# Head sums, low-rank products and a row broadcast as float32r passes of two parts, in a hybrid decoder trunk

## The chip, the cores and the metric

The kernel runs on one core of one Trainium2 chip. The metric is the device time of one execution in microseconds (us); the time before is a median over runs, and the profile is of one further execution.

## The reference

The program is a decoder trunk of two layers over 512 tokens of width 1024. Each layer is half a SwiGLU block, a mixer, and another half of a SwiGLU block; layer 0 mixes with differential attention and RWKV-7, layer 1 with sparse attention (NSA) and an mLSTM. Cut to what the change touches, in float32:

```python
# RWKV-7: 8 heads of 64; the low-rank terms, the normed key, the bonus and the norm of the output
w = -softplus(-(w0 + tanh(wl) @ w2)) - 0.5          # wl: (T, 64), w2: (64, 512)
a = sigmoid(a0 + al @ a2)                           # al: (T, 64), a2: (64, 512)
g = sigmoid(gl) @ g2                                # gl: (T, 128)
kk = kk * rsqrt(sum(kk * kk, over the head) + 1e-12)
S = S * w_t - (S kk) (kk a) + v k                   # state per head, step by step over T
y = (y - mean(y, over the head)) * rsqrt(var(y, over the head) + eps) * ln_w + ln_b
bonus = sum(r * k * r_k, over the head) * v
out = (y + bonus) * g

# mLSTM: 4 heads; each needs its running maximum m (one row of T numbers) on every partition
sqk = (q k) * exp(b_s - b_r + li_r - m_s)
```

## The kernel before

The kernel is written with a tile framework: the program issues instructions in an order of its own, a scheduler reorders them by priority and by modelled times, hands out buffers, and sets all waits. `tc.high_priority(n)` moves a block of instructions n places ahead. Activations lie with channels on the 128 partitions and the 512 tokens along the free axis, so a "512-column matmul" has all tokens as columns.

Nearly all of the work is weight products. `mm3` (L245 to L249) takes a float32 product apart: weights and activations are each split in a high part, rounded to float32r, and a low part, the rest; three float32r passes (high by high, high by low, low by high) are summed in PSUM. The split of weights is `split_weights` (ScalarE copy L275, VectorE subtraction L276). The small products of the mixers are matmuls on plain float32 operands.

Layer 0's mixer is `mix0` (from L685). It handles the eight RWKV heads as four pairs `hp` (two heads fill 128 partitions). `ORDER0` lists the steps: `in` (projections of r, k, v by `shifted`), `prep` (`rwkv_prep`), `inv` (`rwkv_inverse`, a triangular inverse by levels; the next pair's `prep` runs between its levels), `chain` (`rwkv_chain`), `din` and `attn` (differential attention), `out` (output projection). `AHEAD` moves `inv` 200 and `chain` 700 places ahead; the projections, the attention and `out` fill TensorE between their steps.

In `rwkv_prep` the two low-rank products of a pair (64 rows each: L764 on partitions 0 to 63, L768 on 64 to 127) read the tile `wag`, of two buffers, in which three DMAs put a pair's columns of w2, a2 and g2. A sum over a head is a matmul with the 0/1 matrix `blk` (128x128): L792 (squares of the key), L809 (bonus), and in the tail of `rwkv_chain` L963 (mean) and L967 (variance). L811 reads the product of L809 once the pair before has given up its `bonus`. `rwkv_chain` goes through eight chunks of 64 tokens: for each, two state products (L925), an addition (L927), two products (L931), two copies (L932, L933), two products (L937) and the new state (L945), which is kept in the tile `S` of seven buffers until the outputs (L956); `Sq` has the decayed old state (L944). Products take PSUM from the banks of a stream: `pi` (two banks) in `prep` and `inv`, `pc` (one) in `chain`, `mm` (two) in the projections.

`self.temp()` is a ring of three tiles of 128x512 for short-lived values: `shifted` uses one, `diff_in` one for each of q, k, v and one more while `rope` swaps rows by four DMAs (L631).

In layer 1, `mix1_gates` leaves the running maximum of the four mLSTM heads in `fm` (4 x 512), and `mlstm_head` copies a head's row to all 128 partitions by a product with a column of the identity (L1165, four rows).

## Time and profile before

| | us |
|---|---|
| median of 3 runs | 2134.4 |
| lowest and highest of them | 2131.72, 2139.27 |
| the profiled execution | 2132.14 |
| its span in the trace | 2130.3 |

TensorE is busy for 99% of the span, VectorE for 78%, ScalarE for 51%; the granted clock is 0.998 of full speed on average. A busy share counts time in which at least one instruction is under way. Matmuls are pipelined: one that takes 0.39 us can end 0.23 us after the one before it, so what an operation costs TensorE is read from the distance between the ends, not from its duration.

### The profile page before, as it was taken

How to read it: one execution, taken by the hardware profiler on the slowest of the kernel's cores; microseconds unless marked ns; L12 is line 12 of the kernel's file. 1: busy time of each engine (PE TensorE's matmuls, PEld its weight loads, DVE VectorE, ACT ScalarE, POOL GpSimd, SP SyncE). 2: the span in 40 equal slices, each digit the busy share in tenths (PEclk: the TensorE clock that was granted, in tenths of full speed). 3: DMA queues.
4: the chain of work that ended last, by engine and by line, in shares of the span. 5: the costliest groups of instructions: out<-in, count | busy, mean ns of one | idle time of the engine just before them, and what ended most of it. 6: DMA issues, size and time to landing. Idle time of an engine off the chain costs nothing.

```text
span 2130.3 us, 35226 instructions
## 1 busy us (share of the span) xinstructions
PE 2102.7 (99%) x14028; PEld 1787.9 (84%) x14028; DVE 1668.6 (78%) x2824; ACT 1086.3 (51%) x1917; POOL 68.4 (3%) x70
## 2 busy tenths in 40 slices
PE   9999999999999999999999999999999999999998
PEld 7999998776667679999989999997777768999997
DVE  7888886777778798878859787876687867888885
ACT  7544445534434465444446454453368846544444
POOL 1000002000000020000010000001000001000000
PEclk9999999999999999999999999999999999999999
DMA  5333334221121033333323333336421023333331
GB/s 145 106 105 106 103 100 125 69 59 46 43 58 34 31 99 98 116 94 102 107 90 99 106 102 108 95 97 165 120 59 36 25 62 88 97 115 96 102 107 70
DMA packets 306965, 190.94 MB, mean 90 GB/s; under 512 B 20054, under 2 KB 302448, under 8 KB 306800
## 3 DMA queue, kind: packets, MB, share of 16 engines
q1 hardware_dynamic: 305680, 187.59, 30.2%
q8 instruction: 110, 1.80, 0.4%
q0 software_dynamic: 1120, 1.11, 0.3%
q14 instruction: 55, 0.45, 0.1%
HBM read 181.32 MB, written 2.10 MB: 86 GB/s over the span
## 4 chain that ended last, share of the span: by engine, by line
PE 93%; DVE 3%; ACT 2%; DMA 1%; issue 1%; POOL 0%; SPq 0%; DVEq 0%; ACTq 0%; POOLq 0%
PE ps L518 33%; PE ps L247 15%; PE ps L248 15%; PE ps L249 15%; PE ps L849 2%; PE ps L1379 1%; PE ps L831 1%; PE ps L1376 1%; PE ps L1229 1%; DVE wlo L276 1%; PE ps L1182 1%; PE ps L1360 1%; PE ps L1035 1%; PE ps L952 0%; PE ps L1361 0%
## 5 line engine op out<-in xcount | busy, mean ns | idle before, releaser
L275 ACT ACTIVATE whi<-wraw 128x1024 fp32r<-128x1024 f32 (+2 forms) x367 | 320.5, 876 | 307.9 <-PE ps L248 197.3
L276 DVE TENSOR_TENSOR wlo<-wraw,whi 128x1024 fp32r<-128x1024 f32 (+2 forms) x367 | 368.6, 1006 | 75.7 <-ACT whi L275 72.2
L518 PE MATMUL ps<-xi,shi 128*128 128x256 f32 x1800 | 330.6, 283 | 1.4 <-ACT g L529 1.4
L518 PEld LDWEIGHTS ps<-xi,shi 128*128 128x128 f32 x1800 | 280.6, 192 | 1.8 <-ACT g L529 1.8
L248 PE MATMUL ps<-hlo,whi 128*128 128x512 f32 (+1 forms) x716 | 276.9, 387 | 0.0
L247 PE MATMUL ps<-hhi,whi 128*128 128x512 f32 (+1 forms) x716 | 276.8, 387 | 0.0
L249 PE MATMUL ps<-hhi,wlo 128*128 128x512 f32 (+1 forms) x716 | 276.2, 386 | 0.0
L518 PE MATMUL ps<-xi,slo 128*128 128x256 f32 x900 | 254.4, 283 | 0.0
L247 PE MATMUL ps<-xhi,whi 128*128 128x512 f32 x600 | 245.7, 411 | 0.3
L248 PE MATMUL ps<-xlo,whi 128*128 128x512 f32 x600 | 243.4, 406 | 0.4 <-DVE xlo L294 0.4
L249 PE MATMUL ps<-xhi,wlo 128*128 128x512 f32 x600 | 243.0, 405 | 0.0
L501 ACT ACTIVATE shi<-sum 128x1024 fp32r<-128x1024 f32 x150 | 158.5, 1059 | 136.0 <-DVE sum L496 89.1
L502 DVE TENSOR_TENSOR slo<-sum,shi 128x1024 fp32r<-128x1024 f32 x150 | 183.2, 1222 | 29.0 <-ACT shi L501 28.2
L518 PEld LDWEIGHTS ps<-xi,slo 128*128 128x128 f32 x900 | 172.6, 192 | 0.0
L518 PE MATMUL ps<-xlo,whi 128*128 128x256 f32 x600 | 169.6, 283 | 0.0
L518 PE MATMUL ps<-xhi,whi 128*128 128x256 f32 x600 | 169.4, 283 | 0.0
L518 PE MATMUL ps<-xhi,wlo 128*128 128x256 f32 x600 | 169.3, 283 | 0.0
L495 DVE TENSOR_TENSOR sum<-wraw 128x512 f32<-128x512 f32 x150 | 99.1, 689 | 88.1 <-DMA wraw<-in_ffa_up_dram 45.6
L249 PEld LDWEIGHTS ps<-hhi,wlo 128*128 128x128 f32 x716 | 134.5, 188 | 27.3
L247 PEld LDWEIGHTS ps<-hhi,whi 128*128 128x128 f32 x716 | 134.7, 188 | 25.7
L248 PEld LDWEIGHTS ps<-hlo,whi 128*128 128x128 f32 x716 | 134.7, 188 | 24.9
L247 PEld LDWEIGHTS ps<-xhi,whi 128*128 128x128 f32 x600 | 113.6, 190 | 28.3 <-issue 3.8
(422 smaller groups left out, 4198.0 us busy)
## 6 DMA issues: line engine op xcount, KB each, us to landing
wraw<-in_ffb_gate_dram SPq DMA_DIRECT2D x44, 512.0 KB, 3.8
wraw<-in_ffb_up_dram SPq DMA_DIRECT2D x44, 512.0 KB, 3.9
wraw<-in_ffa_gate_dram SPq DMA_DIRECT2D x43, 512.0 KB, 3.8
wraw<-in_ffa_up_dram SPq DMA_DIRECT2D x43, 512.0 KB, 3.9
wraw<-in_ffa_down_dram SPq DMA_DIRECT2D x48, 384.0 KB, 3.1
wraw<-in_ffb_down_dram SPq DMA_DIRECT2D x48, 384.0 KB, 3.1
wraw<-in_ab_w_in_dram SPq DMA_DIRECT2D x26, 512.0 KB, 3.9
wraw<-in_cd_w_in_dram SPq DMA_DIRECT2D x18, 512.0 KB, 3.8
```

Source lines behind the costliest of these rows:

```text
L247: mm(out, w[0], x[0], start=start, stop=False)
L248: mm(out, w[0], x[1], start=False, stop=False)
L249: mm(out, w[1], x[0], start=False, stop=stop)
L275: nc.scalar.activation(h, raw, AF.Copy)
L276: nc.vector.tensor_sub(l, raw, h.bitcast(F32))
L495: nc.vector.tensor_add(t[:, 0], *first)
L501: nc.scalar.activation(hi, t, AF.Copy)
L502: nc.vector.tensor_sub(lo, t, hi.bitcast(F32))
L518: nc.tensor.matmul(out, a[:, j], b, start=first and i + j == 0, stop=i + j == 5, skip_group_check=True)
L831: mm(p[:, c * P:(c + 1) * P], BK[h, 4 * q + c, :], AR[h, 4 * q + c, :], start=True, stop=True)
L849: mm(p[h, c * LC:(c + 1) * LC], lhs[h, c, :], rhs[h, c, :], start=True, stop=True)
L1035: mm(po[:, :P], et[:, j, :], v[:, j, :], start=j == 0, stop=j == i)
```

## The change

`head_sums` replaces the float32 matmuls with `blk` (L792, L809 and, for pairs 0 to 2, L963 and L967): the operand is split in two float32r parts in two tiles of `temp()`, and two float32r passes with a float32r `blk` add up in PSUM. `blk` holds zeros and ones, which a float32r operand holds exactly, so it has one part. Pair 3 keeps the float32 matmuls in its chain. The low-rank products are three float32r passes for each half, of `wr` (w2 and a2 of the pair) split in `w2hi`, `w2lo` and of the activations, split once. g2 goes to a tile of its own. The RWKV states go into columns of `BT` that are done with, and `S`, `Sq`, `wag` and `wa` are dropped. For the mLSTM the four rows of m are split in float32r, high parts on rows 0 to 3 and low parts on rows 32 to 35 of a 64-row tile of zeros, and one float32r pass with a two-ones column `sel` gives the broadcast.

```diff
+    def head_sums(self, p, t):
+        nc = self.nc
+        hi, lo = [self.temp().bitcast(FR) for _ in range(2)]
+        nc.scalar.activation(hi, t, AF.Copy)
+        nc.vector.tensor_sub(lo, t, hi.bitcast(F32))
+        for part in (hi, lo):
+            nc.tensor.matmul(p, self.blk, part, start=part is hi, stop=part is lo)
...
# mix0: blk is loaded apart from the other constants, and rounded
+            blk = self.temp()[:, :P]
+            self.nc.sync.dma_start(blk, a["c_blk"])
+            self.blk = self.tile("blk", (P, P), FR)
+            self.nc.scalar.activation(self.blk, blk, AF.Copy)
...
# rwkv_low
-        wa = self.shifted(6 * T, 12, "wa")
+        wa = self.shifted(6 * T, 12, "rkv")
...
+        hi, lo = [self.tile(n, dt=FR) for n in ("wahi", "walo")]
+        nc.scalar.activation(hi, wa, AF.Copy)
+        nc.vector.tensor_sub(lo, wa, hi.bitcast(F32))
+        return (hi, lo), gl
...
# rwkv_prep
-        wag = R["wag"] = self.tile("wag", (P, 2, P))
-        nc.sync.dma_start(wag[:64, 0, :], self.a["rwkv_w2"][0, :, cs])
-        nc.sync.dma_start(wag[64:, 0, :], self.a["rwkv_a2"][0, :, cs])
-        nc.sync.dma_start(wag[:, 1, :], self.a["rwkv_g2"][0, :, cs])
-        p = self.psum("pi")
-        mm(p, wag[:64, 0, :], wa[:64, :], start=True, stop=True)
-        sig = self.tile("tr")
-        self.act(sig, p, AF.Sigmoid, bias=self.vec("w0", hp))
-        p = self.psum("pi")
-        mm(p, wag[64:, 0, :], wa[64:, :], start=True, stop=True)
-        av = self.tile("tr")
-        self.act(av, p, AF.Sigmoid, bias=self.vec("a0", hp))
+        g2 = R["g2"] = self.tile("g2", (P, P))
+        wr, whi, wlo = self.tile("wr", (P, P)), self.tile("w2hi", (P, P), FR), self.tile("w2lo", (P, P), FR)
+        nc.sync.dma_start(wr[:64], self.a["rwkv_w2"][0, :, cs])
+        nc.sync.dma_start(wr[64:], self.a["rwkv_a2"][0, :, cs])
+        nc.sync.dma_start(g2, self.a["rwkv_g2"][0, :, cs])
+        nc.scalar.activation(whi, wr, AF.Copy)
+        nc.vector.tensor_sub(wlo, wr, whi.bitcast(F32))
+        ps = [self.psum("pi") for _ in HALF]
+        for i, (w_, x) in enumerate(((whi, wa[0]), (whi, wa[1]), (wlo, wa[0]))):
+            for p, h in zip(ps, HALF):
+                mm(p, w_[h], x[h], start=i == 0, stop=i == 2)
+        sig, av = [self.tile("tr") for _ in ps]
...
-        mm(p, K0["blk"], sq, start=True, stop=True)
+        self.head_sums(p, sq)
...
-        mm(p, K0["blk"], r, start=True, stop=True)
+        self.head_sums(p, r)
...
# rwkv_chain
-                S2 = self.tile("S", (P, LC))
+                S2 = BT[:, c, :LC]
...
-                    sd = self.tile("Sq", (P, LC))
+                    sd = BT[:, c - 1, LC:]
...
-        mm(p, K0["blk"], y, start=True, stop=True)
+        if hp < 3:
+            self.head_sums(p, y)
+        else:
+            mm(p, self.blk.bitcast(F32), y, start=True, stop=True)
...
-        mm(p, K0["blk"], q, start=True, stop=True)
+        if hp < 3:
+            self.head_sums(p, q)
+        else:
+            mm(p, self.blk.bitcast(F32), q, start=True, stop=True)
...
# mix1_gates
-        m = self.tile("fm", (4, T))
+        m = self.temp()[:4, :]
...
+        fm, sel = self.tile("fm", (64, T), FR), self.tile("sel", (64, 4), FR)
+        nc.vector.memset(fm.bitcast(F32), 0.0)
+        nc.scalar.activation(fm[:4, :], m, AF.Copy)
+        nc.vector.tensor_sub(fm[32:36, :], m, fm[:4, :].bitcast(F32))
+        nc.vector.tensor_add(sel, self.ident[:64, :4], self.ident[:64, 32:36])
+        return gt, (fm, sel), ccol, mcol
...
# mlstm_head
-        mm(p, self.ident[:4, h:h + 1].to_broadcast([4, P]), m, start=True, stop=True)
+        mm(p, m[1][:, h:h + 1].to_broadcast([64, P]), m[0], start=True, stop=True)
```

## Rows read from the trace of the kernel before

**Rows 1.** Busy us by stretch: length, PE, PEld, DVE, ACT, POOL; PEclk, DMA share, GB/s.

```profile
391.00:744.00 353.00, 348.80 (x3144) 242.91 (x3144) 273.11 (x553) 157.59 (x352) 0.00 (x0) 1.00 0.16 45
1459.00:1745.00 286.00, 283.76 (x1427) 207.43 (x1426) 209.52 (x491) 169.05 (x406) 7.20 (x13) 0.99 0.28 70
760.00:1270.00 510.00, 508.77 (x3362) 468.90 (x3361) 421.14 (x628) 262.67 (x401) 13.73 (x10) 1.00 0.35 102
```

**Rows 2.** TensorE's waits, 391 to 744 us: waiter, releaser, total, times, longest.

```profile
PE ps L809 <- DVE rkv L807: 1.1, 1, 1.1
...
PE ps L249 <- DVE wlo L276: 0.3, 1, 0.3
```

**Rows 3.** Timeline of TensorE (start, duration in us), first low-rank pair.

```profile
390.36 0.39 PE L248 MATMUL ps<-xlo,whi 128*128 128x512 f32 x1
390.59 0.39 PE L249 MATMUL ps<-xhi,wlo 128*128 128x512 f32 x1
390.91 0.69 PE L764 MATMUL ps<-wa,wag 64*128 64x512 f32 x1
390.91 0.69 PE L768 MATMUL ps<-wa,wag 64*128 64x512 f32 x1
...
391.97 0.50 PE L247 MATMUL ps<-xhi,whi 128*128 128x512 f32 x1
```

**Rows 4.** Timeline of the weight loads, same place.

```profile
390.37 0.19 PEld L249 LDWEIGHTS ps<-xhi,wlo 128*128 128x128 f32 x1
```

**Rows 5.** Timeline of TensorE, a head sum in the tail of pair 0's chain.

```profile
486.23 0.40 PE L248 MATMUL ps<-xlo,whi 128*128 128x512 f32 x1
486.46 1.02 PE L963 MATMUL ps<-BV,c_rwkv 128*128 128x512 f32 x2
486.91 0.80 PE L249 MATMUL ps<-xhi,wlo 128*128 128x512 f32 x1
```

**Rows 6.** Timeline of TensorE, the first low-rank product of pair 2.

```profile
494.93 1.12 PE L764 MATMUL ps<-wa,wag 64*128 64x512 f32 x2
```

**Rows 7.** Timeline of TensorE, the broadcast for the last mLSTM head.

```profile
1726.88 0.39 PE L247 MATMUL ps<-nv,whi 128*128 128x512 f32 x1
1727.20 1.12 PE L1165 MATMUL ps<-fm,c_main 4*128 4x512 f32 x2
1728.25 0.50 PE L248 MATMUL ps<-nk,whi 128*128 128x512 f32 x1
```

**Rows 8.** Groups by line: a split of 128x512 (busy us, mean ns | idle before).

```profile
L452 DVE TENSOR_TENSOR hlo<-u,hhi 128x512 fp32r<-128x512 f32 x88 | 60.6, 690 | 5.2 <-ACT hhi L451 2.8
L451 ACT ACTIVATE hhi<-u 128x512 fp32r<-128x512 f32 x88 | 55.2, 628 | 44.7 <-DVE u L540 40.5 <-DVE u L424 3.9
```

**Rows 9.** Instructions on tile BV, 562 to 565.5 us: durations in ns, starts.

```profile
L961 ACT ACTIVATE BV<-ps x1: 597/597/597, 562.4 to 562.4; 128x512 f32<-128x512 f32 x1
L964 DVE SCALAR_TENSOR_TENSOR BV<-ps,BV x1: 680/680/680, 564.5 to 564.5; 128x512 f32<-128x512 f32 x1
```

**Rows 10.** Timeline of all engines, one chunk of pair 3's chain.

```profile
714.00 0.33 PE L925 MATMUL ps<-S,AR 64*64 64x64 f32 x4
...
718.25 0.33 PE L925 MATMUL ps<-S,AR 64*64 64x64 f32 x4
```

**Rows 11.** Line L975, the chain's last; the last filling pass before `out` 3.

```profile
L975 DVE TENSOR_TENSOR ob<-ps,BV x4: 686/690/692, 493.1 to 739.8; 128x512 f32<-128x512 f32 x4
...
743.54 0.40 PE L249 MATMUL ps<-whi,wlo 128*128 128x512 f32 x1
```

**Rows 12.** Instructions on the temp ring (tile t), 560 to 576 us.

```profile
L631 SPq DMA_DIRECT2D t<-t x4: 507/582/590, 563.0 to 564.8; - x4
...
L1000 DVE TENSOR_TENSOR dq<-t,dq x2: 685/686/687, 565.9 to 566.6; 64x512 fp32r<-64x512 f32 x2
```

**Rows 13.** Tile bonus, 480 to 500 us.

```profile
L971 DVE SCALAR_TENSOR_TENSOR BV<-BV,vecs_mix,bonus x1: 752/752/752, 492.3 to 492.3; 128x512 f32<-128x512 f32 x1
L811 DVE TENSOR_TENSOR bonus<-ps,rkv x1: 681/681/681, 493.7 to 493.7; 128x512 f32<-128x512 f32 x1
```

More of the change, by code (lines that the diff above doesn't have):

```diff
@@ L67, in _constants @@
     rwkv = [
-        ("blk", (p[:, None] // LC == c128[None, :] // LC)),
         ("score", np.concatenate([s < t, s <= t], axis=1)),
@@ L74, in _constants @@
     ]
+    blk = [("blk", p[:, None] // LC == c128[None, :] // LC)]
     end = 16 * np.arange(N_CMP) + 31
@@ L85, in _constants @@
     ]
-    return {"main": _pack(main), "rope": _pack(rope), "rwkv": _pack(rwkv), "nsa": _pack(nsa)}
+    return {"main": _pack(main), "rope": _pack(rope), "rwkv": _pack(rwkv), "blk": _pack(blk), "nsa": _pack(nsa)}
 CONST = _constants()
@@ L95 @@
     "ffn": {"xi": NT, "xn": 2, "fr": 2, "g": 2, "u": 2, "hhi": HF, "hlo": HF, "sum": 2, "shi": 2, "slo": 2},
-    "m0": {"rkv": 4, "wag": 2, "tr": 4, "pc": 2, "AR": 2, "Sr0": 2, "Sr1": 2, "X": 3, "Y": 2, "w1": 2, "S": 7, "Sq": 2,
+    "m0": {"rkv": 4, "g2": 2, "tr": 4, "pc": 2, "AR": 2, "Sr0": 2, "Sr1": 2, "X": 3, "Y": 2, "w1": 2,
            "bonus": 1, "dq": 1, "dk": 1, "sm_m": 4, "sm_e": 2, "smT": 1, "z": 4, "ss": 2, "junk": 1},
@@ L743, in rwkv_low @@
         self.act(gl, gl, AF.Sigmoid)
-        return wa, gl
+        hi, lo = [self.tile(n, dt=FR) for n in ("wahi", "walo")]
+        nc.scalar.activation(hi, wa, AF.Copy)
+        nc.vector.tensor_sub(lo, wa, hi.bitcast(F32))
+        return (hi, lo), gl
     def rwkv_in(self, hp):
@@ L756, in rwkv_prep @@
         r, k, v = R["in"]
-        wag = R["wag"] = self.tile("wag", (P, 2, P))
-        nc.sync.dma_start(wag[:64, 0, :], self.a["rwkv_w2"][0, :, cs])
-        nc.sync.dma_start(wag[64:, 0, :], self.a["rwkv_a2"][0, :, cs])
-        nc.sync.dma_start(wag[:, 1, :], self.a["rwkv_g2"][0, :, cs])
-        p = self.psum("pi")
-        mm(p, wag[:64, 0, :], wa[:64, :], start=True, stop=True)
-        sig = self.tile("tr")
-        self.act(sig, p, AF.Sigmoid, bias=self.vec("w0", hp))
-        p = self.psum("pi")
-        mm(p, wag[64:, 0, :], wa[64:, :], start=True, stop=True)
-        av = self.tile("tr")
-        self.act(av, p, AF.Sigmoid, bias=self.vec("a0", hp))
+        g2 = R["g2"] = self.tile("g2", (P, P))
[10 more added lines that the diff above has]
+        sig, av = [self.tile("tr") for _ in ps]
+        self.act(sig, ps[0], AF.Sigmoid, bias=self.vec("w0", hp))
+        self.act(av, ps[1], AF.Sigmoid, bias=self.vec("a0", hp))
         yield
@@ L972, in rwkv_chain @@
         p = self.psum("pc")
-        mm(p, R["wag"][:, 1, :], gl, start=True, stop=True)
+        mm(p, R["g2"], gl, start=True, stop=True)
         out = self.tile("ob")
@@ L1135, in mix1_gates @@
         self.act(mcol, mcol, AF.Exp, scale=-1.0)
-        return gt, m, ccol, mcol
+        fm, sel = self.tile("fm", (64, T), FR), self.tile("sel", (64, 4), FR)
[4 more added lines that the diff above has]
+        return gt, (fm, sel), ccol, mcol
     def mlstm_in(self, i):
```

## The prediction

> **What bounds the kernel now.** I read the granted clock first (0.998, so it explains nothing), then the busy time by stretch, then TensorE's waits, then the timeline. In layer 0's mixer TensorE is busy for 348.8 of 353 us, in layer 1's for 283.8 of 286 [rows 1]; the seven waits listed for the first add up to 3.8 us, from 1.1 to 0.3 us [rows 2]. Busy is not yet bound, so I look at the ends of matmuls: two float32r passes of 512 columns end 0.23 us apart (390.75, 390.98) though each lasts 0.39 [rows 3], and in the mixers such a stream is only broken by other matmuls. TensorE's stream is therefore the first limit, and a pass taken out of it should shorten the mixer.
>
> There is a second limit close behind. The RWKV pairs run strictly one after another from 391 to 740 us: the products of pair 1's inverse can't go on before L811 has freed a bank of `pi`, and L811 (493.7) waits for L971 of pair 0's chain (492.3) [rows 13]. Pair 3's chain ends at 740.5, and the work that fills TensorE beside it ends at 743.9 [rows 11]: only 3.4 us of filling is left over. So the serial path and the stream end almost together, and this is where a gain can leak.
>
> **The change part by part.**
>
> *Head sums, 14 of them* (two in each of four preps, two in the chains of pairs 0 to 2). A float32 sum has two passes: the pass before ends at 486.63, the one behind at 487.71, of which 0.23 is its own, so the sum costs 0.85 us [rows 5]. Two float32r passes cost 0.45 by the distance of [rows 3]. TensorE saves 0.40 us each, 5.6 us in all.
>
> The weight load speaks for that price: it lasts 0.19 us and lies wholly beside the pass before it, on the same 128 rows [rows 4]. The Trainium skill, "TensorE: Matmul & The Clock Gate", Part 3 (what overlaps and what doesn't), says that a load overlaps a matmul in flight only when the row group differs. By that rule a pass would cost 0.42 and the sums would save next to nothing; the trace contradicts it here, and the case is a rival below.
>
> *Low-rank products.* The first pair's two products start together, and from the end before (390.98) to the end of the L247 behind (392.47) less its 0.23 they take 1.26 us together [rows 3]. The other six stand alone: the two passes of one take 1.12 us [rows 6], as the four-row broadcast does, which costs 1.25 with a switch of rows on both sides (1727.27 to 1728.75, less 0.23) [rows 7]. Of that, 0.85 is the passes and 0.40 the two switches. Beside other 64-row work a switch is partly spared, so I take 1.15: 6.9 + 1.26 = 8.1 us. New: three passes for each half. Side by side, as in [rows 3], a pair costs 3 x 0.23 + 0.40 = 1.1 us; one after another 6 x 0.23 + 0.40 = 1.8. For four pairs 4.4 or 7.1 us, a saving of 3.7 or 1.0. I take 3.7, since the new order issues the two halves next to each other, the nearest row.
>
> *mLSTM broadcast, 4 of them.* 1.25 us [rows 7] becomes one pass of 0.23 and, with 64 rows, the same 0.40 of switches: 0.62 saved each, 2.5 us. Bounds: 1.0 each if 64 rows needed no switch, 0.4 if a switch doubled.
>
> TensorE is relieved by 5.6 + 3.7 = 9.3 us in layer 0 and 2.5 us in layer 1, 11.8 us together.
>
> *What is added on the other engines.* A split of 128x512 is 0.63 us of ScalarE and 0.69 of VectorE [rows 8]. Fourteen of them, one for the low-rank activations and four of a quarter of the width are at most 19 x 0.69 = 13 us of VectorE and 12 of ScalarE, against 353 - 273 = 80 and 195 us idle there [rows 1]: hidden as load. In layer 1 a memset, a copy and two small VectorE operations, at most 2 us, run once in the gate step beside projections. The load of `blk` and one small copy run at the start of layer 0 beside projections. The states in `BT` are written where the product L937 of the same chunk has read, which the new state waits for anyway; the next pair's transposes wait for the last state read, but they wait for the bank of `pc` longer still. The low-rank activations take the first slot of `rkv` only until they are split, and the running maximum takes a temp for some 2 us in the gate step. All this I cost at nothing; where VectorE's idle time is not where an operation falls, its 0.69 us comes on the path, which is in the bound of +10 below. A pair's three DMAs on SP's queue stay three. `wr` no longer waits for the chain before, as `wag` did, so these DMAs move earlier; what could queue behind them are weight loads that have three buffers in front.
>
> *What is added on the serial path.* From the end of the copy L961 (563.0) to the reader of its sum (564.5) are 1.5 us now [rows 9]; with ScalarE 0.63, VectorE 0.69, a pass of 0.39 and hops of some 0.4 in all it is about 2.1. Six tail sums and the first pair's key sum lie on the path: 7 x 0.6 = +4.2 us. The low-rank products of pairs 1 to 3 lie on it too and go from about 2.3 to 1.1 us: -3.6. Net about +1 us; bounds -2 (hops hidden) and +10 (below).
>
> *What that makes.* A chunk of a chain takes 4.25 us (714.00 to 718.25) [rows 10]. Its own instructions and hops, without the filling between, are an estimated 2.9 us: three product groups of 0.33, VectorE and ScalarE operations of 0.2 to 0.3 between them, six hops. A chunk without filling is thus some 1.35 us shorter, and leaves about 2.6 us of filling undone: what the filling lacks is given back by half. With a path longer by L, TensorE relieved by 9.3 and 3.4 us left over, the filling lacks L + 5.9. For L = 1 that is 6.9 us, given back 3.6. The chain ends at 740.5 + 1 - 3.6 = 737.9 instead of 740.5, and the output product follows there instead of at 743.9: 6.0 us gained in layer 0. With 2.5 in layer 1 the forecast is -8.5 us.
>
> The profiled execution took 2132.14 us, 2.3 under the median of the runs, 2134.4. Its own sum is 2123.6; against the median, which is what I predict, 2125.9, rounded to 2126.
>
> **The rivals.**
>
> *Nothing leaks.* The scheduler keeps filling beside the last chain and all 11.8 us come through: 2122.6. For it: TensorE hardly waits now [rows 2]. Against: only 3.4 us of filling are over [rows 11]. Chance 0.22.
>
> *The temp ring delays the tails.* A head sum takes two of three temps. In the tail of pair 1 (sum at 563) `din` holds one for q until L1000 ends at 567.3, one for k, and a third for the row swaps issued from 563.0 [rows 12]: both parts would wait about 4 us or more. The tail of pair 2 falls beside a `din` too. With two such tails L is about 10: the filling lacks 15.9, gives back 8.3, the gain in layer 0 is 740.5 + 10 - 8.3 against 743.9, 1.7 us; with 2.5 that is -4.2: 2130. Against: the chain is 700 places ahead and takes a freed temp first. Chance 0.24.
>
> *Slower: the ring on every tail.* All six tail sums wait 5 us each: L = 31. Giving back ends with the chain's eight chunks, 11 us, so layer 0 ends 740.5 + 31 - 11 - 743.9 = 16.6 us later; less 2.5, 2148. It decides from L = 17 for a loss at all and L = 23, some 4 us for each tail sum, for one that can be measured. Against: no `din` holds temps in the tail of pair 0. Chance 0.06.
>
> *The passes don't get cheaper.* If the load of a second pass on the same rows showed after all, a pass would cost 0.42; the sums save nothing, the low-rank products 4 x (2.0 - 1.65) = 1.4 and the broadcast 1.7; with L = 3 the filling lacks 1.0, layer 0 gains 0.9, and 2.6 us in all give 2132. [rows 4] is against it. Chance 0.03.
>
> *The serial path is the bound, and stiff.* The chunks don't shorten without filling. Then the 3.4 us left over and 2.5 of layer 1 are gained, L = 1 to 4 lost: 2130.5. Against: chunks with filling between their groups [rows 10]. Chance 0.12.
>
> **How the numbers follow.** Forecast 0.33, nothing leaks 0.22, two tails 0.24, stiff path 0.12, no cheaper passes 0.03, slower 0.06. The forecast's own range is 2122 to 2129. Left out of the whole range are the slower rival and the outermost of the two fast cases: 2120 to 2134. The runs before spread over 7.5 us, and about 0.3%, 6.4 us, can be told from no change: faster than 2128.0 are nothing leaks, most of the forecast (0.28) and a few of the others (0.06), 0.56; slower than 2140.8 0.06; the rest, 0.38, within.
>
> **What would show it.** Right: `blk` passes 0.23 us apart by their ends; the two halves of a low-rank product with equal starts; the broadcast as one pass; TensorE's busy time in the layer 0 mixer some 6 us less, with the last chain's chunks under 4 us and little filling behind it; layer 1's mixer shorter by 2.5 us. Wrong: TensorE waits for `lo` parts of the sums, gaps before the splits in the tails of pairs 1 and 2, L811 more than 1 us later behind the copy L961 than before, or a last chain with idle TensorE and chunks still over 4 us. If halves run one after another, 2.7 us of the relief are missing. A reordering by the scheduler that this sum can't see would break it anywhere by some us.

## The result and the profile after

The changed kernel is slower: 2215.8 us median (2204.0 to 2221.3) beside 2135.0 for the kernel before, a ratio of 1.0375 (95% interval 1.0358 to 1.0391). The forecast was 2126, the slowest rival 2148. Of the runs before, the bound for "no change" was 6.4 us; this is +80.8 us. The profiled execution (span 2202.1 us) is the quickest of the changed kernel's four; the one before had a span of 2130.3 us, 71.8 less.

The page of the changed kernel shows where at a glance: TensorE's share falls from 99% to 97%, and in two slices, 11 and 12 of 40 (551 to 661 us), the granted clock is 0.6 and the DMA engines move 2 and 11 GB/s.

```profile
PE 2138.8 (97%) x14032; PEld 1824.5 (83%) x14032; DVE 1686.7 (77%) x2846; ACT 1106.3 (50%) x1945; POOL 68.1 (3%) x70
PEclk9999999998669999999999999999999999999999
GB/s 148 112 98 110 94 103 128 61 49 41 2 11 86 30 49 84 108 106 104 95 100 101 99 112 101 94 106 131 142 73 48 30 49 67 108 101 108 106 101 72
```

Measured from the start of the first low-rank matmul to the end of the last one of the chains and of the attention, layer 0's mixer took 349.0 us before and 421.1 after, 72.1 more. From there to the end both need about the same, 1390.4 and 1391.8 us. So the whole loss stands in layer 0's mixer, and nearly every reading below is about it.

The next view is TensorE's busy time by stretch in the changed kernel (columns as in [rows 1]), where that clock falls:

```profile
500.00:535.00 35.00, 31.94 (x361) 24.58 (x359) 28.88 (x53) 19.38 (x38) 0.00 (x0) 1.00 0.22 64
535.00:560.00 25.00, 23.98 (x176) 17.55 (x174) 10.06 (x31) 6.09 (x22) 0.00 (x0) 0.57 0.01 1
560.00:580.00 20.00, 18.46 (x135) 12.03 (x135) 10.68 (x27) 7.67 (x16) 0.00 (x0) 0.50 0.00 1
...
620.00:645.00 25.00, 20.17 (x160) 14.99 (x160) 9.54 (x26) 3.02 (x10) 0.00 (x0) 0.58 0.08 23
645.00:660.00 15.00, 11.02 (x117) 8.71 (x117) 5.59 (x17) 2.80 (x8) 0.00 (x0) 0.50 0.00 0
```

TensorE is listed as busy for 24 of the 25 us from 535 on, and yet this is the sick stretch: the mean clock is 0.57, so for most of it the clock is at 0.5, the 1.2 GHz level. What is missing is seen by asking for one line alone, L247, the first pass of every projection (length, PE, PEld, clock, DMA share, GB/s). In the changed kernel:

```profile
500.00:535.00 35.00, 8.82 (x21) 3.95 (x21) 1.00 0.22 64
535.00:560.00 25.00, 0.00 (x0) 0.00 (x0) 0.57 0.01 1
560.00:580.00 20.00, 0.00 (x0) 0.00 (x0) 0.50 0.00 1
...
620.00:645.00 25.00, 0.00 (x0) 0.00 (x0) 0.58 0.08 23
645.00:660.00 15.00, 0.00 (x0) 0.00 (x0) 0.50 0.00 0
```

And the kernel before in the same stretches:

```profile
535.00:560.00 25.00, 5.37 (x13) 2.14 (x13) 1.00 0.05 11
560.00:580.00 20.00, 5.72 (x12) 2.23 (x12) 1.00 0.26 73
...
620.00:645.00 25.00, 6.61 (x15) 2.82 (x15) 1.00 0.23 64
645.00:660.00 15.00, 3.45 (x8) 1.56 (x8) 1.00 0.11 37
```

Twice, beside chain 1 and beside chain 2, there is no filling by projections at all. What then stands between the chain's groups is other small work: products of the next pair's inverse (L850) and, beside chain 1, pieces of the attention (L679). TensorE's timeline of one chunk of chain 1 and, below the second gap, of one of chain 2 in the changed kernel, to be held against [rows 10]:

```profile
547.76 0.48 PE L944 MATMUL ps<-BT,AR 64*64 64x64 f32 x4
548.17 0.90 PE L679 MATMUL ps<-c_main,sm_e 128*128 128x128 f32 x3
...
549.41 0.79 PE L850 MATMUL ps<-AR,BK 64*128 64x128 f32 x2
...
553.03 0.48 PE L944 MATMUL ps<-BT,AR 64*64 64x64 f32 x4
...
644.38 0.48 PE L944 MATMUL ps<-BT,AR 64*64 64x64 f32 x4
...
647.17 0.48 PE L944 MATMUL ps<-BT,AR 64*64 64x64 f32 x4 [0.24 <-DVE BT L965]
```

The first chunk takes 5.27 us against 4.25 with filling in [rows 10], and the same group of four takes 0.48 us where it took 0.33. The second has no other work of TensorE between its groups and takes 2.79 us, at the same low clock. From the second chunk's start to the eighth's, chain 1 takes 32.2 us (24.6 before) and chain 2 24.6 (28.4 before). So the chains are not where most of the time goes (all four together are 5.6 us longer). It goes behind them: from the start of chain 2's last chunk to that of chain 3's second are 110.3 us, 60.9 before, since the filling that was held back, and all that follows it in the program, is done only then.

Why is there no filling? ScalarE's timeline around the tail of chain 1 in the changed kernel answers it (L741 is the copy of an operand into its high part, in a temp; L732 is the scaled copy of a token shift, in a temp too; L183 the helper through which Exp, Ln and Sigmoid go):

```profile
587.22 0.61 ACT L741 ACTIVATE t<-W 128x512 fp32r<-128x512 f32 x1
587.74 0.71 ACT L732 ACTIVATE t<-pr,vecs_mix 128x512 f32<-128x512 f32 x1
588.47 1.28 ACT L183 ACT_TABLE_LOAD   x1
589.76 0.69 ACT L183 ACTIVATE W<-ps,gneps 128x512 f32<-128x512 f32 x1
590.47 1.28 ACT L183 ACT_TABLE_LOAD   x1
591.76 0.63 ACT L183 ACTIVATE W<-W 128x512 f32<-128x512 f32 x1
```

The projection for the first shift of `in` 3 had been drained into `pr` at 504.7 us. Its scaled copy needs a temp, and runs at 587.74, right behind the high part of the second sum of chain 1's tail; in the kernel before the three copies of `in` 3 ran at 504.8, 520.4 and 529.6:

```profile
L728 ACT ACTIVATE t<-pr,vecs_mix x3: 709/712/725, 504.8 to 529.6; 128x512 f32<-128x512 f32 x3
```

In the program `in` 3 stands behind chain 1, and `din` 1 behind chain 2: the ring of three temps is handed out in that order, so a temp that a tail will need is kept from filling that is ready 80 us earlier. `din` 1's first step, at 553.0 before, came at 664.1, right behind the split of the second sum of chain 2's tail (662.8). And there is a second thing in these lines: two loads of an activation table stand in the tail, which the tail before did not have. The experiments take the two apart, and find a third: the steps of the split themselves come late.

### The profile page after: what moved, and what is told of

It reads as the page before. It is cut to its first block, busy times and chain, and to the rows that moved or that the text cites. A ratio compares the mean times of both kernels' runs of the same rounds, so it can differ in the third digit from the quotient of the medians.

```text
span 2202.1 us, 35309 instructions
## 1 busy us (share of the span) xinstructions
PE 2138.8 (97%) x14032; PEld 1824.5 (83%) x14032; DVE 1686.7 (77%) x2846; ACT 1106.3 (50%) x1945; POOL 68.1 (3%) x70
## 4 chain that ended last, share of the span: by engine, by line
PE 89%; DVE 5%; ACT 3%; DMA 2%; issue 1%; POOL 0%; SPq 0%; DVEq 0%; POOLq 0%; ACTq 0%
PE ps L518 32%; PE ps L247 14%; PE ps L248 14%; PE ps L249 14%; PE ps L868 2%; PE ps L850 1%; PE ps L1411 1%; PE ps L1408 1%; DVE wlo L276 1%; PE ps L972 1%; PE ps L744 1%; ACT whi L275 1%; PE ps L950 1%; PE ps L1061 1%; PE ps L1261 1%
## 5 line engine op out<-in xcount | busy, mean ns | idle before, releaser
L275 ACT ACTIVATE whi<-wraw 128x1024 fp32r<-128x1024 f32 (+2 forms) x367 | 320.4, 875 | 328.7 <-PE ps L248 216.6
L276 DVE TENSOR_TENSOR wlo<-wraw,whi 128x1024 fp32r<-128x1024 f32 (+2 forms) x367 | 368.6, 1006 | 80.7 <-ACT whi L275 77.2
L247 PE MATMUL ps<-hhi,whi 128*128 128x512 f32 (+1 forms) x716 | 276.8, 387 | 0.0
L249 PE MATMUL ps<-hhi,wlo 128*128 128x512 f32 (+1 forms) x716 | 276.2, 386 | 0.0
L247 PE MATMUL ps<-xhi,whi 128*128 128x512 f32 x600 | 245.5, 411 | 0.1
L249 PE MATMUL ps<-xhi,wlo 128*128 128x512 f32 x600 | 241.9, 404 | 0.0
L249 PEld LDWEIGHTS ps<-hhi,wlo 128*128 128x128 f32 x716 | 134.5, 188 | 27.2
L247 PEld LDWEIGHTS ps<-hhi,whi 128*128 128x128 f32 x716 | 134.7, 188 | 25.7
L247 PEld LDWEIGHTS ps<-xhi,whi 128*128 128x128 f32 x600 | 114.5, 191 | 27.3 <-issue 3.5
```

The source lines that it names most:

```text
L247: mm(out, w[0], x[0], start=start, stop=False)
L249: mm(out, w[1], x[0], start=False, stop=stop)
L275: nc.scalar.activation(h, raw, AF.Copy)
L276: nc.vector.tensor_sub(l, raw, h.bitcast(F32))
```

## The experiments

All differences below are against the runs of the kernel before on the same chip. The expectations call some kernels by short names: all_own is the one without temps in any sum, no_sums the one with every sum float32, own_brake and nosums_brake the same two with an order on ScalarE, low_wag the second with the old tile, and own_wag, prep_wag and tail_wag its three successors. "Mixer" is the length of layer 0's mixer, taken as above from each kernel's profiled execution. What lies behind the mixer is not compared between profiles: it is 3.9 us longer in the states_only kernel, whose layer 1 is that of the kernel before and whose time is the same.

### Is it the ring of temps?

Three kernels take the ring away in part or whole, and one brings it into the kernel before. First, the tails' parts in tile `UV`, which a tail no longer needs (the preparations' sums still take temps):

```
+        uv = self.halves(self.tile('UV', (P, NCH, P), FR))
-            self.head_sums(p, y)
+            self.head_sums(p, y, uv)
...
-            self.head_sums(p, q)
+            self.head_sums(p, q, uv)
```

> The changed kernel with one thing undone: the two parts of the sums in a chain's tail stand in the two halves of the tile UV, which the chain is done with, instead of in two temps; the splits, their two hops and the float32r passes stay. Theory ring (temps go out in the order of the program, so every projection behind a chain waits for the chain's tail, the chain runs without filling, and the clock falls): the mixer of layer 0 falls from 421 us to 350 to 360 and the time to 2125 to 2140, with the clock at full speed. Theory latency (the split's hops lengthen the serial path): nothing changes, 2190 or more. Theory states or buffers (states in BT, the shared slot of rkv, the two banks taken at once): nothing changes, 2190 or more.

Measured: 2174.8 us, 1.0184 (1.0154 to 1.0215), +39.5 us; mixer 381.0. Half of the loss is gone. `in` 3's shifts are drained by 537, but `din` 1 is still late (609): it stands behind the sums of pair 3's preparation.

Second, the tails' sums float32 again:

```
-        if hp < 3:
+        if hp < 0:
```

> The changed kernel with the sums of all tails as float32 matmuls again; the sums of the preps, the low-rank products, the states in BT and the broadcast stay as changed. Theory ring: 2125 to 2140, since the tails take no temps. Theory latency: also down, to 2130 to 2150. Theory states or buffers: 2190 or more.

Measured: 2179.3 us, 1.0200 (1.0176 to 1.0224), +44.0; mixer 393.1. Without any part in a tail the preparations' temps, with what the change does besides, keep 44 us; the second cause below is 16 of them.

Third, the kernel before with only the ring's use added, four one-column temps in each of the tails of pairs 0 to 2, everything else as it was:

```
+        for s_ in (y, y) if hp < 3 else ():
+            nc.scalar.activation(self.temp()[:, :1], s_[:, :1], AF.Copy)
...
+        for s_ in (q, q) if hp < 3 else ():
+            nc.scalar.activation(self.temp()[:, :1], s_[:, :1], AF.Copy)
```

> The kernel before, with all its float32 sums, and in the tails of pairs 0 to 2 four temps that are taken and hold one column copied from the operands of the sums, 0.2 us of ScalarE each. Theory ring: most of the loss comes back without any of the change, 2180 to 2215. Theory latency: 2135 to 2139. Theory states or buffers: 2135 to 2139.

Measured: 2182.5 us, 1.0213 (1.0194 to 1.0232), +47.2; mixer 398.5. Twelve copies of one column, 0.28 us each in the trace, cannot cost 47 us by themselves. The ring alone does it: two shifts of `in` 3 are drained only at 570.2 and 573.8 (519.7 and 528.4 before), `din` 1's first step comes at 641, no pass of L247 runs between 540 and 560, and the granted clock is 0.50 there. The chains themselves are 3.1 us shorter than before, added up as above; the whole loss stands between chains 2 and 3, 110.2 us here as in the changed kernel (all_own below: 66.2).

Fourth, no temp in any sum: tails in `UV`, the key sums in `BK` before it is filled, the bonus sums in two `tr` tiles:

```
-        self.head_sums(p, sq)
+        self.head_sums(p, sq, self.halves(self.tile('BK', (P, NCH, P), FR)))
...
-        self.head_sums(p, r)
+        self.head_sums(p, r, [self.tile('tr', dt=FR) for _ in HALF])
```

> The changed kernel without temps in any sum: tails in UV, the key sums of the preps in the tile BK before it is filled, the bonus sums in two tiles of tr. Theory ring: the waits of the preps' sums go too, 2 to 6 us under tail_uv, 2120 to 2135, so faster than the kernel before if the relief of TensorE comes through. Theory latency: 2190 or more, like tail_uv. Theory states or buffers: 2190 or more.

Measured: 2154.9 us, 1.0088 (1.0072 to 1.0104), +19.6; mixer 367.3. Of the 80.8 us, 61 were the ring's. The other 20 are not.

A fifth run, made later, leaves the sums' temps where they are and takes the shifts' temp out of the ring instead:

```
-        t = self.temp()
-        nc.scalar.activation(t, pr[:, :T], AF.Copy, scale=self.vec("mu", row))
         out = self.tile(name)
-        nc.vector.scalar_tensor_tensor(out, pr[:, 1:], self.mu1[:, row:row + 1], t, op0=ALU.mult, op1=ALU.add)
+        nc.scalar.activation(out, pr[:, :T], AF.Copy, scale=self.vec("mu", row))
+        nc.vector.scalar_tensor_tensor(out, pr[:, 1:], self.mu1[:, row:row + 1], out, op0=ALU.mult, op1=ALU.add)
```

> The changed kernel with the temp of every token shift taken out of the ring of three: the scaled copy is written into the output tile and the second step works in place. The parts of the sums, and the temps of the attention's q, k and v projections (din), stay in the ring. Theory 'temps go out in program order': the shifts of in 3 no longer stand behind the sums of tail 1 and are drained before 545 us (587.7 in the changed kernel), so chain 1 is filled again; din 1 comes after chain 2 in the program and still stands behind the sums of tails 1 and 2, so chain 2 stays unfilled. Part of the 61 us between all_own and the changed kernel comes back, the rest does not: 2175 to 2200. Rival 'the sums are late because of their own two splits, whoever takes the temps': within 2205 to 2220, as the changed kernel.

Measured: 2200.9 us, 1.0317 (1.0298 to 1.0335), +65.4; mixer 414.9. In the trace it went as the theory of the ring says: `in` 3 is drained at 511.5, 528.1 and 538.2, chain 1's beginning is fed (535 to 560 us at clock 1.00), `din` 1 comes at 659, and from 580 to 645 no pass of L247 runs. In time only 15 us came back, a hair outside the expected range. Chain 1 takes 26.0 us instead of 32.2, but between chains 2 and 3 there are 110.8 us still: what costs most is `din` 1, and it was not freed. A ring of more than three tiles was not tried.

### What are the other 20 us? The wait that was lost

In the kernel before, `wag` had two buffers and held w2, a2 and g2, so that the loads for pair 2 waited until chain 0's gate product had read g2. The change gave w2 and a2 a tile of their own, `wr`, and nothing holds them back any more. The kernel before with that alone:

```
-        wag = R["wag"] = self.tile("wag", (P, 2, P))
+        wr = self.tile("wr", (P, P))
+        g2 = R["g2"] = self.tile("g2", (P, P))
```

> The kernel before with one thing changed: w2 and a2 of a pair lie in a tile of their own (two buffers) and g2 in another (two buffers), so that the low-rank products of pair 2 no longer wait until the gate product of chain 0 has read the tile. All arithmetic, sums, temps and states are those of before. Theory 'lost brake': the sigmoids of pairs 2 and 3 move ahead of the tails of chains 0 and 1 on ScalarE, the activation table changes more often (18 or so loads of 1.28 us between 385 and 815 us where before had 9), attention and tails come later: 2145 to 2157, which is what all_own still had over before. Rival 'the low-rank products come earlier and nothing else happens': 2132 to 2136, as before.

Measured: 2150.8 us, 1.0078 (1.0059 to 1.0096), +15.5; mixer 365.1. No arithmetic differs. ScalarE's timeline shows what happens at the end of chain 0 in this kernel:

```profile
469.91 1.28 ACT L183 ACT_TABLE_LOAD   x1
471.20 0.69 ACT L183 ACTIVATE tr<-ps,vecs_mix 128x512 f32<-128x512 f32 x1
...
493.94 1.28 ACT L183 ACT_TABLE_LOAD   x1
495.24 0.69 ACT L183 ACTIVATE W<-ps,gneps 128x512 f32<-128x512 f32 x1
495.94 1.28 ACT L183 ACT_TABLE_LOAD   x1
497.24 0.63 ACT L183 ACTIVATE W<-W 128x512 f32<-128x512 f32 x1
```

The same place in the kernel before:

```profile
490.09 0.69 ACT L183 ACTIVATE W<-ps,gneps 128x512 f32<-128x512 f32 x1 [0.52 <-PE ps L967]
490.81 0.63 ACT L183 ACTIVATE W<-W 128x512 f32<-128x512 f32 x1
...
495.18 1.28 ACT L183 ACT_TABLE_LOAD   x1
496.48 0.69 ACT L183 ACTIVATE tr<-ps,vecs_mix 128x512 f32<-128x512 f32 x1
```

Pair 2's Sigmoid ran at 496.48 behind the tail; now it runs at 471.20 in the middle of the chain, its table load with it, and the tail's Ln (495.24) and Exp (497.24) each need a load in front. Between 385 and 815 us there are 18 loads where there were 9; from 545 to 556 us Sigmoids of pair 3 and Exps of the attention take turns, with a load ahead of each. The head that attends beside the chains ends late (tile `oa` at 572.0 instead of 565.1), and with it the output product that fills TensorE next (first result at 600.7 instead of 577.2).

The Trainium skill, "ScalarE: Activation LUTs" (What ACT_TABLE_LOAD costs), states about 1.28 us for a load, as measured here, and (Table sets) that a Ln followed by an Exp needs one load, since one set holds both. The trace differs on the second: in a tail behind a Sigmoid each of the two has its own. Only where the set with both was loaded ahead of them (L190), as in the tail before, does neither have one.

The changed kernel with all sums float32 tests the same from the other side:

```
-        self.head_sums(p, sq)
+        mm(p, self.blk.bitcast(F32), sq, start=True, stop=True)
...
-        self.head_sums(p, r)
+        mm(p, self.blk.bitcast(F32), r, start=True, stop=True)
...
-        if hp < 3:
+        if hp < 0:
```

> The changed kernel with all 16 head sums of layer 0 as float32 passes again, so without temps and without parts; low-rank products, states in BT and the broadcast stay as changed. Theory 'lost brake': the sigmoids of pairs 2 and 3 are still free to move ahead, so 2143 to 2160, no better than all_own. Rival 'the parts of the sums are what remains': 2126 to 2134.

Measured: 2151.1 us, 1.0083 (1.0062 to 1.0104), +15.8; mixer 360.8, 18 table loads. With no split sum left the loss is about that of the lost wait alone.

Then the wait was put back, first as an order on ScalarE, into the kernel without temps and into the one without split sums (`first` is the copy of `wr` into its high part, `done` the last Exp of a tail):

```
-        nc.scalar.activation(whi, wr, AF.Copy)
+        first = nc.scalar.activation(whi, wr, AF.Copy)
+        if hp >= 2:
+            self.behind(first, [self.done[hp - 2]])
```

> all_own (the changed kernel whose head sums take no temps) with one ordering edge on ScalarE added: the copy of wr into its high part, for pair 2 and 3, stands behind the last Exp of the tail two pairs back, so that the low-rank stage waits about as long as it did before. Theory 'lost brake': table loads fall back to 9 between 385 and 815 us, the layer-0 mixer loses the 18 us that all_own had over before, and the relief of TensorE shows: 2122 to 2132. Rival 'the parts of the sums (two more instructions each on ScalarE and VectorE) are what remains': 2145 to 2155, as all_own (2155).

Measured: 2164.1 us, 1.0141 (1.0120 to 1.0162), +28.8; mixer 371.5. A miss: 9 table loads, as expected, and yet 9 us slower than without the order. In this kernel the tail of pair 0 ends at 505.6 (493.1 before), the low-rank stage of pair 2 follows it, and the attention, whose Exps stand behind that stage's table load, starts at 512.4 instead of 500.8. Something else made the tail late, and the wait handed it on.

> no_sums (all head sums float32, low-rank products, states and broadcast as changed) with the ordering edge that puts the low-rank stage of pairs 2 and 3 behind the last Exp of the tail two pairs back on ScalarE. Theory 'lost brake, and own_brake was late because the parts of the sums delay tail 0 and with it the table load that attention 0 stands behind': 9 table loads between 385 and 815 us, tail 0 done at 493 to 499 us, first attention Exp at 500 to 505, oa of head 0 near 566, time 2128 to 2138. Rival 'the brake is not the cause, or the low-rank products and the states cost by themselves': 2145 to 2160, as no_sums.

Measured: 2143.8 us, 1.0043 (1.0028 to 1.0058), +8.2; mixer 354.3. Half of the 15.8 came back, less than expected. Tail 0, first Exp and `oa` were where they should be (497.1, 503.2, 568.3). What remained is a place in the order of VectorE and ScalarE. The low parts of the weights of the first output product, the filling that comes next, are made in the kernel before at

```profile
567.93 1.22 DVE L276 TENSOR_TENSOR wlo<-wraw,whi 128x1024 fp32r<-128x1024 f32 x1
573.99 1.22 DVE L276 TENSOR_TENSOR wlo<-wraw,whi 128x1024 fp32r<-128x1024 f32 x1
```

and in this kernel, behind the steps of pair 3's preparation, at

```profile
583.94 1.21 DVE L276 TENSOR_TENSOR wlo<-wraw,whi 128x1024 fp32r<-128x1024 f32 x1
593.09 1.22 DVE L276 TENSOR_TENSOR wlo<-wraw,whi 128x1024 fp32r<-128x1024 f32 x1
```

The high part of the first was there at 572.4; that of the second stood in ScalarE's queue behind such steps too, until 587.2. Each of TensorE's third passes (L249) waits for the low parts, and the product's first result came at 597.5 instead of 577.2. So the lost wait is shown as a cause, but what share of its 15.5 us the table loads have is not: this kernel has the 9 loads of before and still half of the loss. I took this first for a late load, since SP asks for the next weights only at 585 (569 before), and that stands in the next expectation; but SP waits there for L276 to free the buffer, and the weights of the output product had landed long before. So the tile of the kernel before was put back whole, in the kernel without split sums:

```
-        g2 = R["g2"] = self.tile("g2", (P, P))
-        wr, whi, wlo = self.tile("wr", (P, P)), self.tile("w2hi", (P, P), FR), self.tile("w2lo", (P, P), FR)
+        wag = R["wag"] = self.tile("wag", (P, 2, P))
+        wr, g2 = wag[:, 0, :], wag[:, 1, :]
+        whi, wlo = self.tile("w2hi", (P, P), FR), self.tile("w2lo", (P, P), FR)
```

> no_sums (sums float32; low-rank products, states and broadcast as changed) with w2, a2 and g2 in one tile of two buffers again, as in the kernel before, so that the loads of pair 2 and 3 wait on SP for the gate product two pairs back, at the place in SP's queue where they stood before. Theory 'lost brake': 2126 to 2137 and 9 table loads between 385 and 815 us; what nosums_brake still had over before (8 us, out 0's weights asked for at 585 us against 569) was the place of the loads in SP's queue. Rival 'the low-rank passes themselves cost, by their order or the two added copies': 2141 to 2150, as nosums_brake and no_sums.

Measured: 2137.8 us, 1.0030 (1.0020 to 1.0039), +5.9; mixer 350.6, 9 table loads. The wait in its old place gives 10 of the 15.8 us back. The low parts of the output weights come at 575.8 and 583.6 here, still 8 and 10 us later than before, and the product's first result at 586.7. The time is a hair above the expected range. Of the 5.9 us the mixer has 1.7, and the broadcast of the mLSTM, which this kernel has too, 2.0 by its own run below; the rest is open. What is left is no gain either, though TensorE was relieved: its busy time in the mixer is 342.03 us here and 344.86 in the kernel before (349.0 us long, clock 1.00).

```profile
388.10:738.80 350.70, 342.03 (x3124) 237.54 (x3124) 270.71 (x547) 153.05 (x348) 0.00 (x0) 1.00 0.15 45
```

### Do split sums pay where nothing stands in their way?

Three kernels on that base: all 14 sums split with no temps, only the preparations' eight, only the tails' six. The edits are those of the first group.

> low_wag with 14 split head sums whose parts lie in tiles that are not in use (tails in UV, key sums in BK, bonus sums in two tr tiles): no temps from the ring, and the loads of w2, a2 and g2 wait as in the kernel before. Theory 'the ring and the lost brake were all': 14 sums x 0.40 us of TensorE less, 2128 to 2138. Rival 'each split sum makes its stage later by its two parts, about 1.2 us against 0.4 us saved, and the fixed order turns that into missing filling': 2142 to 2162.

Measured: 2163.1 us, 1.0134 (1.0117 to 1.0152), +28.9; mixer 373.6.

> low_wag with only the 8 sums of the preparations split, their parts in BK and tr, the tails' sums float32. Theory 'the ring and the lost brake were all': 2130 to 2138. Rival 'the parts make a stage later': the preparation of pair 0 has nothing beside it and delays the whole chain, so most of own_wag's loss is here: 2140 to 2155.

Measured: 2150.0 us, 1.0073 (1.0052 to 1.0093), +15.9; mixer 358.3.

> low_wag with only the 6 sums of tails 0 to 2 split, their parts in UV, the preparations' sums float32. Theory 'the ring and the lost brake were all': 2130 to 2138. Rival 'the parts make a stage later': chains run beside filling, a later tail costs little as long as filling lasts: 2134 to 2145.

Measured: 2142.8 us, 1.0038 (1.0022 to 1.0054), +8.6. (The profiled execution was its slowest, 2150.7, so its mixer of 360.1 is not used.) Its interval overlaps that of low_wag, 1.0020 to 1.0039, so the tails' six sums alone cost little that can be told from nothing.

The theory that ring and lost wait were all falls. Without either, the sums that were to bring 5.6 us cost 23 us more than float32 sums (28.9 less 5.9). The preparations alone cost 10.0 of them and the tails alone 2.7; the other 10 come only with both. Both single kernels lie in the range of the rival, and the whole just above it. The first steps of the reason are seen in the very first sum. In the kernel with all sums split (L809 writes the operand, L741 and L742 make the parts, L744 is a pass, L275 and L276 split weights for projections):

```profile
399.10 0.71 ACT L809 ACTIVATE tr<-rkv,vecs_mix 128x512 f32<-128x512 f32 x1
...
399.71 1.04 ACT L275 ACTIVATE whi<-wraw 128x1024 fp32r<-128x1024 f32 x1
...
400.66 0.62 ACT L741 ACTIVATE BK<-tr 128x512 fp32r<-128x512 f32 x1
400.78 1.23 DVE L276 TENSOR_TENSOR wlo<-wraw,whi 128x1024 fp32r<-128x1024 f32 x1 [1.12 <-ACT whi L275]
...
401.93 0.68 DVE L742 TENSOR_TENSOR BK<-tr,BK 128x512 fp32r<-128x512 f32 x1
...
402.82 0.39 PE L744 MATMUL ps<-BK,blk 128*128 128x512 f32 x1
...
403.25 0.69 ACT L183 ACTIVATE tr<-ps,mu 128x512 f32<-128x512 f32 x1 [1.37 <-PE ps L744]
```

The kernel before:

```profile
397.50 0.71 ACT L790 ACTIVATE tr<-rkv,vecs_mix 128x512 f32<-128x512 f32 x1
...
398.26 1.13 PE L792 MATMUL ps<-tr,c_rwkv 128*128 128x512 f32 x2 [0.55 <-ACT tr L790]
...
399.67 0.68 ACT L183 ACTIVATE tr<-ps,gneps 128x512 f32<-128x512 f32 x1
```

From the end of the operand to the reader of the sum are 3.44 us instead of 1.46: +2.0, where 0.6 was reckoned. The two new steps are as long as they were priced (0.62, 0.68). Each of them stands here in the queue of its engine behind a weight split of filling, 1.04 and 1.23 us long. Of this kernel's ten key and tail sums the high part starts at once behind its operand in eight, behind a weight split in two; the low part starts behind another VectorE instruction in eight, three of them weight splits. No part is seen waiting for its tile. Read in the same way over all pairs (end of the operand's writer to start of the reader, us, pairs 0 to 3; the tail of pair 3 is not split):

| sum | before | all split, no temps (own_wag) | changed kernel |
|---|---|---|---|
| key | 1.46 1.41 2.12 1.31 | 3.45 3.24 4.07 2.53 | 3.45 3.31 4.48 5.63 |
| tail, y | 1.38 1.50 1.62 1.33 | 3.09 2.18 1.99 1.53 | 7.01 3.30 2.27 1.46 |
| tail, q | 1.22 1.38 1.59 1.27 | 1.98 3.57 3.06 1.22 | 1.98 3.96 2.27 1.22 |

How these few us each become 23 was not traced to its end. Of the 24.6 us by which this mixer is longer than before, 3.8 are in the chains' chunks and 17.3 between one chain and the next.

### The two small parts

The states in `BT`, alone in the kernel before:

```
-                S2 = self.tile("S", (P, LC))
+                S2 = BT[:, c, :LC]
...
-                    sd = self.tile("Sq", (P, LC))
+                    sd = BT[:, c - 1, LC:]
```

> The kernel before with only the states of the chain moved into BT (S2 in the first half of a chunk's BT, the decayed copy in the second half of the chunk before). The forecast costed this edit at nothing: 2133 to 2138. Rival 'the states in BT make the chain wait for readers of BT': 2140 or more.

Measured: 2133.3 us, 1.0006 (0.9997 to 1.0016); mixer 349.0. As forecast, nothing.

The broadcast of the mLSTM, alone in the kernel before:

```
-        mm(p, self.ident[:4, h:h + 1].to_broadcast([4, P]), m, start=True, stop=True)
+        mm(p, m[1][:, h:h + 1].to_broadcast([64, P]), m[0], start=True, stop=True)
```

> The kernel before with the mLSTM broadcast alone as one float32r pass of 64 rows (4 per kernel) in place of two float32 passes of 4 rows. The recorded sum gave 4 x 0.62 = 2.5 us of relief to layer 1, so 2132 to 2133.5 by that; if the relief is lost in waits of the head, 2135 to 2137.

Measured: 2137.3 us, 1.0012 (1.0003 to 1.0022), +2.0. The expected 2.5 us did not come. The pass itself is what [rows 7] let expect (one of 0.49 us listed instead of two of 0.64), and TensorE's busy time over the heads, from the first to the last, falls by 1.2 us, from 97.08 to 95.91. But that stretch is 98.1 us long, as it was (98.0). Relief that TensorE gets there becomes waiting; what bounds the heads instead was not tried. Where the 2 us that were lost are was not found: with identical code up to the gate step the traces put the first broadcast anywhere from 182 to 189 us behind the first compression.

## Why the prediction was wrong

Three steps failed. The temp ring was named but priced at some 4 us for a tail; it holds 61 of the 80.8 us. The wait that went with the tile `wag` was costed at nothing; it is 15.5 us by itself. And the seven sums on the serial path were put at +4.2 us; they took 9.2 with no temps in the way. The parts follow in the order of the prediction.

*What bounds the kernel.* "TensorE's stream is therefore the first limit, and a pass taken out of it should shorten the mixer" is the step on which all else rests, and it does not hold. [rows 1] had TensorE busy for 348.8 of 353 us; with low-rank passes taken out, float32 sums and the tile in its old place (low_wag) TensorE is busy 2.8 us less, and the mixer is 1.7 us longer. The same shows in the mLSTM heads: 1.2 us less busy, and no shorter. A busy share of 99% was read as a bound; it is as well what filling laid under every wait looks like. That the limit was instead the serial path, with filling that comes to it in time, fits all runs but is not shown by one of its own: in low_wag the output product is still 9.5 us later than before, with the low parts of its weights 8 and 10 us later on VectorE, so the order had not come back whole.

*Head sums.* The price of a pass was right (in the kernel with all sums split the second pass of the first sum ends at 403.21, the pass of L249 behind it at 403.45). The rule of the Trainium skill weighed there, "TensorE: Matmul & The Clock Gate", Part 3 (what overlaps and what doesn't), is contradicted here too: the weight load for that pass (402.67 to 402.86) lies beside a pass on the same rows (402.59 to 402.99). The 5.6 us were paid with more than that on the other engines.

*Low-rank products.* Pair 0 came side by side as forecast from [rows 3], with three starts for six passes 0.34 and 0.24 apart; in the mid-chain order of the later pairs it did not. TensorE's timeline of the changed kernel:

```profile
389.21 0.50 PE L786 MATMUL ps<-wahi,w2hi 64*128 64x512 f32 x2
389.55 0.40 PE L786 MATMUL ps<-walo,w2hi 64*128 64x512 f32 x2
389.79 0.40 PE L786 MATMUL ps<-wahi,w2lo 64*128 64x512 f32 x2
...
473.32 0.49 PE L786 MATMUL ps<-wahi,w2hi 64*128 64x512 f32 x1
...
478.24 0.49 PE L786 MATMUL ps<-wahi,w2hi 64*128 64x512 f32 x1
```

In pair 2 one half stands at 473.3 and the other at 478.2, so the changed kernel did not have the whole of the 3.7 us taken. With the wait back in its old place (low_wag) the halves of pairs 0, 2 and 3 start together, and TensorE is 2.8 us less busy. A small error beside the others.

*Added work on the other engines, "hidden as load".* It is hidden as load, and that was the wrong question. VectorE's idle 80 us did not help an operation that its fixed order put behind a 1.23 us weight split. The bound of +10 had room for this; the value taken did not.

*"`wr` no longer waits for the chain before, as `wag` did, so these DMAs move earlier."* Seen, and costed at nothing, with only the loads in mind. What moves with them is the whole low-rank stage and its Sigmoid: 15.5 us by itself. The reckoning followed the moved step only as far as its DMAs.

*Serial path.* "7 x 0.6 = +4.2 us" is the mis-sized term. By the table the same seven sums cost 9.2 us more than before with no temps in the way (2.0 for the key, 2.8 for the y sums, 4.4 for the q sums), and 14.1 in the changed kernel. The key sums of pairs 1 to 3, taken to be off the path, add 5.0 and 8.6. The -3.6 us set against them for the low-rank products of pairs 1 to 3 did not come either: from first pass to last they are 0.2, 0.9 and 0.3 us shorter in low_wag.

*"What the filling lacks is given back by half."* The size of a bare chunk was right: put at 2.9 us, it took 2.79 and 2.94 in two chunks of chain 2 with nothing or little between, and that at the lower clock. But the chunks give back next to nothing beside what the lack costs. In chain 1 other small work stood in the gaps and the chunks got longer (5.27 us in the one shown); in the kernel with only the ring's use added all chains together give back 3.1 us. Against that stand the 49 us more between chains 2 and 3, for the filling that had to be done there instead. The sum had filling left over only at the end, where 3.4 us decide; it had no term for filling that is ready and held back.

*The temp ring.* The mechanism was named as a rival and mis-read twice. "The chain is 700 places ahead and takes a freed temp first" holds for the order of work, not for the ring, which goes in program order: `in` 3 and `din` 1, which stand behind a chain in the program, waited for its tail. And the delay was priced as some 4 us for a tail; the tail y of pair 0 did wait (7.01 us to its reader), but the price is the filling held back, `in` 3 for 83 us behind its projection and `din` 1 for 111 us against before, `din` 1 above all. That is 61 of the 80.8 us in the changed kernel, 47.2 alone in the kernel before.

The parts do not add up as a plain sum: without temps, splitting the sums adds 3.8 us where the loads run free (19.6 less 15.8) and 23 where they wait (28.9 less 5.9). A kernel in which a lost wait and late sums stand together (all_own, 2154.9) is not slower than one with late sums and the wait (own_wag, 2163.1); by the trace of own_brake the wait then hands the tail's lateness on to the attention. No kernel of these was faster than the kernel before.

## What to carry to other kernels

A TensorE share of 99% in a mixer with a long serial chain can mean that filling is in place, and need not mean that TensorE is the limit: ask what holds the filling, temps and buffers first, before pricing a pass. A temp from a shared ring is a place in the program's order; one taken in a step that ends late keeps it from every later step that is ready early. A tile split in two, or given a buffer more, takes a wait away, and the wait may be what kept the users of two activation tables apart.

## What was not expected of the hardware

With no projection passes between its groups TensorE fell to the 1.2 GHz level while it was listed as busy for 24 of 25 us (535 to 560 us, granted clock 0.57; the stretch before had 31.94 of 35 at 1.00). The listed busy share did not tell this; the clock column and the count of filling passes did. And in a tail behind a Sigmoid a Ln and an Exp each had a table load of 1.28 us: 2.6 us of ScalarE in a tail that had none before.
